# The parts of the recurrent block's weights are made beforehand and kept in DRAM

## The chip, the cores and the metric

The kernel runs on one core of one Trainium2 chip. TensorE (PE) multiplies, VectorE (DVE), ScalarE (ACT) and GpSimd (POOL) work on elements, and SyncE (SP) issues nearly all DMAs, in the order in which they stand in its queue. The metric is the device time of one execution in microseconds (us).

## The reference

Two decoder layers on 512 tokens of 1024 features, in float32. Layer 0 is half a SwiGLU feed-forward, attention, half a feed-forward; layer 1 has a recurrent block (RWKV-7) in place of attention:

```python
for layer in range(DEPTH):                                  # DEPTH = 2
    x = x + 0.5 * swiglu(rms_norm(x, ...), w_gate, w_up, w_down)      # w_*: 1024 x 2816
    h = rms_norm(x, mix_norm[layer])
    x = x + (attention(h, ...) if layer % 2 == 0 else rwkv7_time_mix(h, ...))
    x = x + 0.5 * swiglu(rms_norm(x, ...), ...)

# rwkv7_time_mix
xx = previous_token(h) - h
xr, xw, xk, xv, xa, xg = [h + xx * mix[i] for i in range(6)]
r, k, v = xr @ w_r, xk @ w_k, xv @ w_v                      # each 1024 x 1024
decay = exp(-exp(-softplus(-(w0 + tanh(xw @ w1) @ w2)) - 0.5))
a, g = sigmoid(a0 + (xa @ a1) @ a2), sigmoid(xg @ g1) @ g2
S_t = S_{t-1} (diag(decay_t) - kk_t^T (kk_t a_t)) + v_t k_t^T;  y_t = S_t r_t
return (group_norm(y) + bonus) * g @ w_o
```

## The kernel before

**Stages.** Six stages run one after the other: feed-forward (0,0), attention, feed-forward (0,1), feed-forward (1,0), the recurrent block, feed-forward (1,1). In the trace the first feed-forward takes the time from the start to about 375 us, the recurrent block that from about 1,382 to 1,860 us.

**Weights as parts.** A float32 product is made of three float32r products: each operand is cut into a high and a low part, and `mm3` issues high x high, high x low, low x high (lines 209 to 211). For each piece of weights `_load` issues the DMA into a raw buffer, and `_conv` casts it on ACT (line 181, the high part) and subtracts on DVE (line 182, the low part). A feed-forward piece is 128 partitions x 1,024 columns, 512 KB; a piece of the recurrent block is 128 x 512, 256 KB. There are 4 raw slots and 4 slots for parts. `next_w` hands out the next block of pieces, having converted up to `conv_ahead` (2) pieces beyond it and loaded as far beyond that as there are raw slots. The recurrent block has 75 pieces: the loras' weights `w1`, `a1`, `w2`, `a2`, `g1`, `g2`; two halves of `wk`, `wv` and `wr` of 8 pieces each; 16 pieces of `wo`. The pieces that stay on for long have slots of their own (`wkeep`).

**The recurrent block's front.** `rwkv` normalizes x chunk by chunk (line 967), takes the difference to the previous token (line 1040) and mixes it on DVE (lines 982 and 992), cuts the result on ACT (line 1000) and POOL (line 1001), and multiplies. In the first half of `wk` two loras run along, so each of 8 chunks has three mixes. Then come the second half of `wk`, `wv` with a third lora, `wr`; between them DVE and POOL prepare the heads (`rw_prep`) and DVE inverts triangular blocks (`rw_inverse`). The recursion over 8 chunks of tokens, the group norm and the output product follow.

**Order.** A scheduler sets the order of each engine's instructions from the data they depend on, their place in the program and its own estimate of times. Each engine then runs its queue in that order, and an instruction that waits holds up all behind it. SP's DMAs use 8 semaphores in turn, so a DMA is issued once the eighth before it has landed.

Of the kernel before, what the change touches and what calls it, by code (L numbers as in the profile page):

```python
# [11 lines left out]
F32 = mybir.dt.float32  # L12
# [7 lines left out]
P = 128  # L20
# [10 lines left out]
# pieces of weights on chip: columns, and how many at a time, as they come and as parts  # L31
# [3 lines left out]
# function tables that serve a function, the first where none of them is there  # L35
# [8 lines left out]
class Trunk:  # L44
    def __init__(self, ctx, tc, aps):
# [6 lines left out]
        # constants, x by chunks of features, and weights as they come  # L52
# [8 lines left out]
        # blk[i, j] = 1 within a head  # L61
# [5 lines left out]
        # pieces that stay on for long, and where  # L67
        self.wkeep = {}
        self.wload = self.wconv = self.wpos = 0
# [3 lines left out]
        self.last_mm = self.turned = self.gate = None  # L73
        self.lo_engine = nc.vector
        self.table, self.table_ins, self.preload = None, [], None

    def act(self, out, in_, func, **kw):
        """An activation; those of one function table stay together."""
        nc = self.nc
        serve = TABLES[func]  # L80
        nosync = mybir.DependencyInfo(mybir.DependencyClass.NoSync, mybir.DependencyReason.DATA)
        if self.table not in serve:
            ins = nc.scalar.preload_act_table_set(serve[0])
            for i in self.table_ins:
                self.tc.add_manual_dep(ins.ins, i.name, nosync, reason="table")
            self.table, self.table_ins, self.preload = serve[0], [ins.ins], ins.ins
        ins = nc.scalar.activation(out, in_, func, **kw)  # L87
        self.tc.add_manual_dep(ins.ins, self.preload.name, nosync, reason="table")
        self.table_ins.append(ins.ins)
        return ins  # L90

    def after(self, ins, dep):
        """ins is not to be issued before dep, which it does not depend on."""
# [15 lines left out]
    def c(self, name, shape, v=None):  # L109
        """A constant or scratch that stays."""  # L110
# [25 lines left out]
    def plan(self, *pieces):  # L136
        """A block of pieces, each a list of (first row, first column, [rows, k, c] source)."""
# [4 lines left out]
    def plan_cols(self, w, c0, c1, step=4):  # L142
        """Columns c0..c1 of w, its rows in chunks of 128, some chunks a piece."""
# [3 lines left out]
    def _load(self, i):  # L147
        tag = self.wring[i]
        cols, slots = RINGS[tag]
        if i and "r" in (tag, self.wring[i - 1]) and tag != self.wring[i - 1]:  # L150
            # the last of the other kind's pieces may be there yet
            self.n_load = 0 if tag == "r" else 2
        c0 = self.n_load % slots * cols
        t = self.raw_all[:, c0 : c0 + cols]
        self.n_load += 1
        for r0, c0, src in self.wlist[i]:
# [3 lines left out]
        self.wraw[i] = t  # L160

    def _conv(self, i):
        n = max(c0 + src.shape[1] * src.shape[2] for _, c0, src in self.wlist[i])
        r = max(r0 + src.shape[0] for r0, _, src in self.wlist[i])
        raw = self.wraw.pop(i)[:r]
# [4 lines left out]
        if i not in self.wkeep:  # L170
            # the smaller pieces take the second half in turn, and those that stay the first
# [8 lines left out]
        hi, lo = parts[:, 0, :], parts[:, 1, :]  # L180
        self.nc.scalar.copy(hi[:r, :n], raw[:, :n])  # L181
# [3 lines left out]
        self.wcv[i] = (hi, lo)  # L185

    def prefetch(self, upto, loads=1 << 30):
        """Pieces converted up to and with this one, and loaded as far ahead as there is room."""
# [10 lines left out]
    def next_w(self):  # L199
        """The next block as a list of (high, low) pieces."""  # L200
        i, n = self.wblocks[self.wpos]
        self.wpos += 1
        self.prefetch(i + n - 1 + self.conv_ahead)
        return [self.wcv.pop(j) for j in range(i, i + n)]

    def mm3(self, out, lhs, rhs, start, stop):
        """out (+)= lhs^T rhs, both given as (high, low) float32r parts."""
# [33 lines left out]
    def name_vectors(self, t):  # L241
        """Values by feature, their chunks on columns."""
# [56 lines left out]
    def rms_prep(self, gain):  # L299
        """High and low parts of x * gain, chunk by chunk."""  # L300
# [14 lines left out]
    def rsqrt(self, out, src, scale, eps, t):  # L315
        """out = (src * scale + eps) ** -0.5: exp and ln, then a Newton step; t is scratch."""
# [6 lines left out]
    def newton(self, t, y, src, scale, eps):  # L323
        """t = -0.5 (src * scale + eps) y^2: 1.5 more and it is the step's factor"""
# [42 lines left out]
    def part(w, k, i):  # L367
        """Columns i * 128.. of chunk k, of pieces of four chunks by 256 columns."""
# [3 lines left out]
    def ffn(self, gain, done=lambda c: None):  # L372
# [6 lines left out]
        def gu(b):  # L379
            ps = [self.bank("b", 8) for _ in range(4)]  # L380
            head = 6 if b == 0 else 0
            if head:
                # chunk by chunk as x comes
# [88 lines left out]
    def attn_setup(self):  # L472
        """Masks, selections, and the relative bias as [query, key] tiles."""
        nc = self.nc
        # tri[j, s] = -1 where j >= s
# [5 lines left out]
        # norm weights, one copy per head of a pair; the logits' scale rides on q's  # L481
# [9 lines left out]
    def attn_tables(self):  # L491
        nc = self.nc
        # selections between natural blocks and classes (token 4l + r)
# [13 lines left out]
        # bias: each head's values by distance, then skewed through DRAM  # L507
# [20 lines left out]
    def attn(self, gain):  # L528
# [5 lines left out]
        def scales():  # L534
            st["rstd"] = self.rms_rstd(ssum)
            # the same per token on partitions: natural blocks, then classes
# [8 lines left out]
        def project(w):  # L545
            """A tile of [128 features, tokens] by one piece of weights."""
# [5 lines left out]
        def project_v(by_class, evac):  # L552
            """Tiles of [128 tokens, 256 features]: natural blocks or classes of tokens."""
# [13 lines left out]
        # stick-breaking heads  # L567
# [27 lines left out]
        # dilated heads  # L595
        vd = {}

        def evac_dv(g):
            def f(b, ps, r):
                # of a pair of heads: V, ones, V  # L600
# [59 lines left out]
    def stick(self, q, k, vs, h, out):  # L660
        """One stick-breaking head in [key, query] tiles; a tile covers the queries from its keys on."""
# [3 lines left out]
        for kb in range(3, -1, -1):  # L665
# [9 lines left out]
            # only keys before the query  # L675
# [25 lines left out]
    def dilated(self, t, qk):  # L701
        """Heads 2t and 2t + 1 of the three groups: one softmax over their keys together, by key."""
# [6 lines left out]
        for e in range(2):  # L709
            j, r = 2 * t + e, slice(e * 64, (e + 1) * 64)  # L710
            # group 0: natural blocks, each with the block before it
# [19 lines left out]
            # groups 1 and 2: classes of tokens  # L731
# [11 lines left out]
        def parts(i, src):  # L743
            """High and low parts, and their sum: what the exchange brings across exactly."""
# [5 lines left out]
        # the maximum over all three, by class and by block  # L750
# [43 lines left out]
    def dilated_out(self, t, pts, vd):  # L794
        nc, mm = self.nc, self.nc.tensor.matmul
        dl = self.row("dlo")
        for e in range(2):
# [9 lines left out]
            # V carries ones beside it, which sum the weights  # L807
# [7 lines left out]
    def plan_rwkv(self):  # L815
# [4 lines left out]
        def half(w, h):  # L820
            """512 columns, a chunk of rows a piece."""
# [30 lines left out]
    def rwkv_setup(self):  # L852
# [7 lines left out]
        # sigmoid(z) = (1 + tanh(z / 2)) / 2  # L860
# [8 lines left out]
        # rows i of both halves: i < t, then i <= t  # L869
# [8 lines left out]
        # 0 where a chunk starts  # L878
        self.runs = self.c("runs", [NC, C], 1.0)
        nc.gpsimd.memset(self.runs[:, :, 0:1], 0.0)  # L880
        # a pair's two heads among the 8 of four pairs: sums over a head's features
# [7 lines left out]
    # partitions of values of 8 heads of either four pairs: the keys' norms, the bonus, the group norm  # L889
# [3 lines left out]
    def rwkv_tables(self):  # L893
        """From the 8 heads of four pairs back to their features."""
# [8 lines left out]
        # hidden layers of the loras (2, 2, then all of the rest's products in one), values of heads (2), that table  # L903
# [5 lines left out]
    def head_sums(self, srcs, scales, squares):  # L909
        """Sums of squares over the features of each of 8 heads."""  # L910
# [8 lines left out]
    def head_scale(self, ps, free, scale, eps, floor=None):  # L919
        """(ps * scale + eps) ** -0.5 for sums [8 heads, tokens], as high and low parts."""  # L920
        nc = self.nc
        ss, y, t = (z[:8] for z in free)
        if floor is not None:
            nc.vector.tensor_scalar(out=ss, in0=ps, scalar1=floor, scalar2=None, op0=ALU.max)
            # the logarithm's range does not reach down to the floor
# [16 lines left out]
    def head_spread(self, n, m):  # L942
        """A pair's values per head on all features of the head."""
# [6 lines left out]
    def rwkv(self, gain):  # L950
# [11 lines left out]
        # h in x's place  # L962
# [14 lines left out]
        def mixed(i, c, tag="xm", bufs=9, dh=None):  # L977
            """High and low parts of h (1 - mix[i]) + (previous token's h) mix[i]."""
# [16 lines left out]
            if tag == "xr":  # L995
                # where a lora's weights were
# [21 lines left out]
        def evac_v(half, ps):  # L1018
            # The recursion is linear in V's features, and the group norm takes their mean off what
            # comes of it: it is taken off V. The bonus has V as it is.  # L1020
# [14 lines left out]
        def less(t, c, ts):  # L1035
            """The previous token's h less this one's."""
# [7 lines left out]
        def started():  # L1044
            """Half of the tokens at a time: the first chunk, and products on it."""
# [14 lines left out]
        def project(half, xm, evac, natural, i_mix=None, loras=(), wl=None):  # L1060
            """Half of a projection's columns, the chunks of rows outermost."""
# [71 lines left out]
        # mix rows: r, w, k, v, a, g  # L1133
# [20 lines left out]
        # the receptances' mix is made twice: there is no room to keep it  # L1154
# [9 lines left out]
        # high, high, low: against high, low, high parts  # L1164
# [9 lines left out]
    def rw_norm(self, sg):  # L1174
        """Norms of the keys' directions, bounded below by 1e-12."""
# [6 lines left out]
    def rw_prep_all(self, sg):  # L1182
        """Four pairs of heads, their steps in turn."""
        # a pair: [kk P(t-1), later y | r P(t) | [k / P, -kk a / P] (2) | ties, later inverse]
# [5 lines left out]
    def rw_prep(self, m):  # L1190
        """Scaled k, kk and kk * a of a pair of heads, and what a chunk's tokens owe each other."""
# [18 lines left out]
        # decay = exp(-exp(-1/2) sigmoid(z)); its products within a chunk, and their inverses  # L1210
# [8 lines left out]
        # the key's direction, -kk / 2; k (1 + (a - 1) ka); -kk a  # L1219
# [18 lines left out]
        # [k / P, -kk a / P], k in its head's half of the rows to come  # L1238
# [6 lines left out]
        # the keys' ties to later directions within a chunk, rows i in the half that is not the head's own  # L1245
# [9 lines left out]
        # the 32-blocks on the diagonal go out for inversion  # L1255
# [11 lines left out]
    def rw_prep2(self, sg):  # L1267
        """The receptances' part of it: r P, and each head's bonus."""
# [309 lines left out]
```

## Time and profile before

| | |
|---|---|
| time, median of 3 runs | 2236.47 us (2234.1 to 2237.83) |
| profiled execution, first to last instruction | 2236.3 us |
| PE busy | 2160.0 us (97%) |
| DVE busy | 1223.1 us (55%) |
| ACT busy | 784.1 us (35%) |
| POOL busy | 283.1 us (13%) |
| moved by DMA | 204.21 MB, mean 91 GB/s |

The profile is of one execution. Its span of 2236.3 us is 0.2 us from the median of the runs, and no separate time of that execution stands beside it. Busy time of PE is not PE at its peak: matmuls are pipelined, so of two products on PE the number of them in a stretch says more than the busy time. The granted clock (PEclk) is 1.00 where the chip lets TensorE run at 2.4 GHz, and 0.50 would be 1.2 GHz throughout.

### The profile page before, as it was taken

The numbers are of one execution on the slowest core, as the hardware profiler recorded it, in microseconds if no ns is written. First come the engines' busy times: TensorE is split into PE (matmuls) and PEld (weight loads), VectorE is DVE, ScalarE is ACT, GpSimd is POOL, SyncE is SP. The second block draws the span as 40 slices with busy tenths as digits, with TensorE's granted clock in tenths as the row PEclk, the third lists the DMA queues.
The fourth block names the chain that finished last, engine by engine and source line by source line (L and its number), as shares of the span: only waits on it lengthen the run. The fifth ranks groups of instructions, "written<-read, shape, count | busy, mean of one in ns | idle before, by whom it ended". The sixth has DMA issues, their size and how long they took to land. (4 is left out here: it accounts for less than half of the span.)

```text
span 2236.3 us, 28431 instructions
## 1 busy us (share of the span) xinstructions
PE 2160.0 (97%) x11489; PEld 1737.6 (78%) x11489; DVE 1223.1 (55%) x1618; ACT 784.1 (35%) x1223; POOL 283.1 (13%) x286
## 2 busy tenths in 40 slices
PE   8999999999999999999999998789888999999999
PEld 6888887768988888888888886566657767888887
DVE  5444445467385444446444445999876456444443
ACT  4322324454234222224222224465533334322222
POOL 3000001120010000001000002663461101000000
PEclk9999999999899999999999998999988899999999
DMA  5232333411023333233232332123423232232322
GB/s 173 76 113 93 97 100 97 119 38 52 20 71 102 99 97 109 76 113 94 77 116 90 103 104 86 47 85 115 128 66 89 61 113 85 82 116 85 109 90 66
DMA packets 229868, 204.21 MB, mean 91 GB/s; under 512 B 39651, under 2 KB 215931, under 8 KB 229736
## 3 DMA queue, kind: packets, MB, share of 16 engines
q1 hardware_dynamic: 227624, 200.29, 30.2%
q10 hardware_dynamic: 2112, 2.10, 0.3%
q8 instruction: 90, 1.47, 0.3%
q14 instruction: 42, 0.34, 0.0%
HBM read 188.68 MB, written 15.51 MB: 91 GB/s over the span
## 5 line engine op out<-in xcount | busy, mean ns | idle before, releaser
L182 DVE TENSOR_TENSOR parts<-const,parts 128x1024 fp32r<-128x1024 f32 (+2 forms) x394 | 428.8, 1094 | 350.2 <-ACT parts L181 341.0
L181 ACT CAST parts<-const 128x1024 fp32r<-128x1024 f32 (+2 forms) x394 | 357.4, 910 | 573.9 <-PE b L210 469.6
L210 PE MATMUL b<-xg,parts 128*128 128x512 f32 x1408 | 549.2, 390 | 0.0
L209 PE MATMUL b<-xg,parts 128*128 128x512 f32 x1408 | 547.0, 391 | 1.6 <-ACT xg L308 1.1
L211 PE MATMUL b<-xg,parts 128*128 128x512 f32 x1408 | 548.3, 390 | 0.0
L209 PEld LDWEIGHTS b<-xg,parts 128*128 128x128 f32 x1408 | 264.7, 188 | 57.7 <-ACT xg L308 1.5
L210 PEld LDWEIGHTS b<-xg,parts 128*128 128x128 f32 x1408 | 264.9, 188 | 56.4 <-issue 1.0
L211 PEld LDWEIGHTS b<-xg,parts 128*128 128x128 f32 x1408 | 264.7, 188 | 55.4 <-DVE parts L182 0.3
L211 PE MATMUL b<-act,parts 128*128 128x512 f32 x704 | 273.3, 389 | 0.0
L210 PE MATMUL b<-act,parts 128*128 128x512 f32 x704 | 273.2, 389 | 0.0
L209 PE MATMUL b<-act,parts 128*128 128x512 f32 x704 | 272.4, 390 | 0.0
L296 POOL TENSOR_TENSOR ssum<-ssum,sq 128x512 f32<-128x512 f32 x41 | 59.2, 1445 | 1191.4 <-ACT sq L295 526.5
L426 DVE SCALAR_TENSOR_TENSOR const<-b,const 128x512 f32<-128x512 f32 x128 | 87.3, 687 | 124.5 <-PE b L211 124.5
L211 PEld LDWEIGHTS b<-act,parts 128*128 128x128 f32 x704 | 132.2, 188 | 27.4
L210 PEld LDWEIGHTS b<-act,parts 128*128 128x128 f32 x704 | 132.2, 188 | 27.4
L209 PEld LDWEIGHTS b<-act,parts 128*128 128x128 f32 x704 | 132.2, 188 | 27.2
L411 DVE TENSOR_TENSOR u<-b,rstd 128x512 f32<-128x512 f32 x88 | 60.4, 690 | 167.1 <-PE b L211 166.9
L214 ACT CAST act<-u 128x512 fp32r<-128x512 f32 x88 | 54.6, 622 | 268.6 <-DVE u L412 268.6
L87 ACT ACTIVATE g<-g 128x512 f32<-128x512 f32 x88 | 55.0, 629 | 188.0 <-DVE g L406 188.0
L406 DVE TENSOR_TENSOR g<-b,rstd 128x512 f32<-128x512 f32 x88 | 60.4, 691 | 108.1 <-PE b L211 107.8
L215 DVE TENSOR_TENSOR act<-u,act 128x512 fp32r<-128x512 f32 x88 | 60.6, 689 | 37.2 <-ACT act L214 36.7
L412 DVE TENSOR_TENSOR u<-u,g 128x512 f32<-128x512 f32 x88 | 60.5, 691 | 2.7
(356 smaller groups left out, 2728.0 us busy)
## 6 DMA issues: line engine op xcount, KB each, us to landing
const<-in_ffn_w_gate_dram SPq DMA_DIRECT2D x88, 512.0 KB
const<-in_ffn_w_up_dram SPq DMA_DIRECT2D x88, 512.0 KB
const<-in_ffn_w_down_dram SPq DMA_DIRECT2D x64, 512.0 KB
const<-in_ffn_w_down_dram SPq DMA_DIRECT2D x48, 256.0 KB
const<-in_attn_w_in_dram SPq DMA_DIRECT2D x24, 512.0 KB
const<-in_rw_wk_dram SPq DMA_DIRECT2D x16, 256.0 KB
const<-in_rw_wv_dram SPq DMA_DIRECT2D x16, 256.0 KB
const<-in_rw_wr_dram SPq DMA_DIRECT2D x16, 256.0 KB
```

The lines of the kernel that those rows point to most:

```text
L87: ins = nc.scalar.activation(out, in_, func, **kw)
L181: self.nc.scalar.copy(hi[:r, :n], raw[:, :n])
L182: self.lo_engine.tensor_tensor(out=lo[:r, :n], in0=raw[:, :n], in1=hi[:r, :n].bitcast(F32), op=ALU.subtract)
L209: self.after(mm(out, lhs[0], rhs[0], start=start, stop=False), self.gate)
L210: mm(out, lhs[0], rhs[1], start=False, stop=False)
L211: self.last_mm = mm(out, lhs[1], rhs[0], start=False, stop=stop)
L215: self.nc.vector.tensor_tensor(out=lo, in0=t, in1=hi.bitcast(F32), op=ALU.subtract)
L296: nc.gpsimd.tensor_tensor(out=ssum, in0=ssum, in1=sq, op=ALU.add)
L406: nc.vector.tensor_tensor(out=g, in0=ps[i], in1=rstd, op=ALU.mult)
L411: nc.vector.tensor_tensor(out=u, in0=ps[2 + i], in1=rstd, op=ALU.mult)
L412: nc.vector.tensor_tensor(out=u, in0=u, in1=gs[i], op=ALU.mult)
L426: nc.vector.scalar_tensor_tensor(out=self.x[c], in0=ps, scalar=0.5, in1=self.x[c], op0=ALU.mult, op1=ALU.add)
```

## The change

A new pair of steps, called parking here, takes the 75 pieces two by two. `park` loads two pieces into a buffer of its own (`praw`), cuts them into parts in another (`pparts`) with one cast on ACT (line 200) and one subtraction on DVE (line 201), and stores high and low parts to DRAM, one DMA a piece (line 204). Both buffers are double. `next_w` calls it at every second block while the flag `parking` is set, in stages 2 and 3. In the recurrent block `_load` does nothing, and `_conv` issues one DMA of 512 KB that brings both parts into their slot (line 226); no cast and no subtraction is left there. All else of the diff is comments taken out. (In the rows of order below, lines of the changed kernel are its own: 167 is the load that was 159, 230 the subtraction that was 182, 1031 the mix that was 982.)

```diff
+        self.parked_w, self.park_ops, self.park_turn = {}, [], 0
+        self.parking = False
     def _load(self, i):
         tag = self.wring[i]
+        if tag == "r":
+            return
...
+    def plan_parks(self, every):
+        small = [i for i, tag in enumerate(self.wring) if tag == "r"]
+        self.park_ops = [small[j : j + 2] for j in range(0, len(small), 2)]
+        self.park_every = every
+    def park_some(self):
+        self.park_turn += 1
+        if self.park_ops and self.park_turn % self.park_every == 0:
+            self.park(self.park_ops.pop(0))
+    def park(self, which):
+        nc = self.nc
+        raw, parts = self.t("praw", [2, S], 2), self.t("pparts", [2, 2, S], 2, F32R)
+        dr = self.dram.tile([len(which), P, 2, S], F32, name=f"parts{which[0]}")
+        spans = []
+        for q, i in enumerate(which):
+            self._fill(i, raw[:, q])
+            spans.append(self._extent(i))
...
+        for r, q, c in spans:
+            hi, lo, src = parts[:r, 0, q, c], parts[:r, 1, q, c], raw[:r, q, c]
+            nc.scalar.copy(hi, src)
+            nc.vector.tensor_tensor(out=lo, in0=src, in1=hi.bitcast(F32), op=ALU.subtract)
+        for q, i in enumerate(which):
+            r, n = self._extent(i)
+            nc.sync.dma_start(dr[q, :r, :, :n], parts[:r, :, q, :n].bitcast(F32))
+            self.parked_w[i] = dr[q, :r, :, :n]
     def _conv(self, i):
...
+        if i in self.parked_w:
+            self.nc.sync.dma_start(parts[:r, :, :n].bitcast(F32), self.parked_w.pop(i))
+            return
+        raw = self.wraw.pop(i)[:r]
         self.nc.scalar.copy(hi[:r, :n], raw[:, :n])
     def next_w(self):
         self.prefetch(i + n - 1 + self.conv_ahead)
+        if self.parking:
+            self.park_some()
...
+    t.plan_parks(2)
     for i in range(start, stop + 1):
+        t.parking = i in (2, 3)
```

SP's queue in the first feed-forward, before, from the third block of columns to the first `down` loads (`const` holds the raw slots):

```order
L159 DMA const<-in_ffn_w_gate_dram 128x4x256 x2
L159 DMA const<-in_ffn_w_up_dram 128x4x256 x2
L159 DMA const<-in_ffn_w_gate_dram 128x4x256 x2
L159 DMA const<-in_ffn_w_up_dram 128x4x256 x2
L159 DMA const<-in_ffn_w_down_dram 128x4x256
L159 DMA const<-in_ffn_w_down_dram 128x2x256
```

The same place now, from the `gate` loads of the fourth block of columns to the first `down` load (`parts_` with a number is a pair's place in DRAM):

```order
L167 DMA const<-in_ffn_w_gate_dram 128x4x256 x2
L204 DMA parts_5181<-pparts 256x1x512 x2
L167 DMA praw<-in_rw_wk_dram 128x512 x2
L204 DMA parts_5302<-pparts 256x1x512 x2
L167 DMA praw<-in_rw_wk_dram 128x512 x2
L167 DMA const<-in_ffn_w_up_dram 128x4x256 x2
L204 DMA parts_5441<-pparts 256x1x512 x2
L167 DMA praw<-in_rw_wk_dram 128x512 x2
L167 DMA const<-in_ffn_w_down_dram 128x4x256
```

The parking, written in stages 2 and 3, depends on nothing that comes before them, and the scheduler has moved all 38 pairs into stage 0: the first load of a pair is number 17 in SP's queue, and the last store stands between the 54th and the 55th of that stage's 72 weight loads.

DVE's queue in the first half of `wk`, before, over two of the 8 chunks:

```order
L982 SCALAR_TENSOR_TENSOR mx<-dh,const 128x512
L182 TENSOR_TENSOR parts<-const,parts 128x512
L982 SCALAR_TENSOR_TENSOR mx<-dh,const 128x512
L967 SCALAR_TENSOR_TENSOR const<-const,rstd 128x512
L182 TENSOR_TENSOR parts<-const,parts 128x512
L982 SCALAR_TENSOR_TENSOR mx<-dh,const 128x512 x2
L1039 TENSOR_SCALAR dh<-const 128x1
L1040 TENSOR_TENSOR dh<-const 128x511
L182 TENSOR_TENSOR parts<-const,parts 128x512 x2
```

The same stretch now:

```order
L1031 SCALAR_TENSOR_TENSOR mx<-dh,const 128x512 x2
L1016 SCALAR_TENSOR_TENSOR const<-const,rstd 128x512
L1031 SCALAR_TENSOR_TENSOR mx<-dh,const 128x512
L1088 TENSOR_SCALAR dh<-const 128x1
L1089 TENSOR_TENSOR dh<-const 128x511
L1031 SCALAR_TENSOR_TENSOR mx<-dh,const 128x512 x2
```

The conversions are gone and the mixes follow each other; the rest of the order is nearly the same.

ACT's queue at the very start holds casts of the parking ahead of the last chunks of x (now; `xg` is x times the gain, line 357):

```order
L357 ACTIVATE xg<-b,const 128x512
L344 ACTIVATE sq<-const 128x512
L200 CAST pparts<-praw 128x1024
L357 ACTIVATE xg<-b,const 128x512
L344 ACTIVATE sq<-const 128x512
```

Before, the two pairs of rows followed each other there, without the cast.

## Rows read from the trace of the kernel before

**Rows 1.** Busy time by stretch (us; PE, PEld, DVE, ACT, POOL, PEclk, DMA share, GB/s)
```profile
40.00:340.00 300.00, 300.00 (x1326) 248.38 (x1325) 137.24 (x168) 84.11 (x102) 0.00 (x0) 1.00 0.33 99
1382.00:1440.00 58.00, 36.59 (x139) 25.77 (x139) 57.02 (x66) 21.70 (x38) 41.31 (x26) 0.84 0.16 50
1440.00:1480.00 40.00, 40.00 (x151) 25.27 (x150) 31.16 (x38) 34.42 (x60) 18.52 (x13) 0.97 0.24 70
1480.00:1580.00 100.00, 84.12 (x430) 59.99 (x428) 95.75 (x148) 47.38 (x78) 51.37 (x36) 0.94 0.36 111
1580.00:1620.00 40.00, 38.94 (x389) 29.22 (x390) 29.97 (x38) 27.88 (x47) 20.23 (x16) 0.89 0.48 125
1720.00:1860.00 140.00, 132.01 (x1337) 97.96 (x1338) 75.47 (x113) 55.60 (x132) 14.65 (x16) 0.90 0.29 86
```

**Rows 2.** Groups on DVE by form, 40 to 340 us (busy, mean ns | idle before)
```profile
L182 DVE TENSOR_TENSOR parts<-const,parts 128x1024 fp32r<-128x1024 f32 x48 | 58.7, 1223 | 66.4 <-ACT parts L181 66.4
L182 DVE TENSOR_TENSOR parts<-const,parts 128x512 fp32r<-128x512 f32 x12 | 8.2, 682 | 0.0
```

**Rows 3.** Groups on DVE and POOL by form, 1,382 to 1,620 us
```profile
L182 DVE TENSOR_TENSOR parts<-const,parts 128x512 fp32r<-128x512 f32 x46 | 45.5, 994 | 6.3 <-ACT parts L181 5.9
...
L1001 POOL TENSOR_TENSOR xl<-mx,xl 128x512 fp32r<-128x512 f32 x16 | 26.0, 1639 | 2.6 <-ACT xl L1000 2.6
```

**Rows 4.** Line 182 alone in five of the stretches (DVE busy, PEclk, DMA share, GB/s)
```profile
1382.00:1440.00 58.00, 11.94 (x8) 0.84 0.16 50
1440.00:1480.00 40.00, 10.47 (x11) 0.97 0.24 70
1480.00:1580.00 100.00, 19.01 (x20) 0.94 0.36 111
1580.00:1620.00 40.00, 7.87 (x10) 0.89 0.48 125
1720.00:1860.00 140.00, 16.88 (x22) 0.90 0.29 86
```

**Rows 5.** The stretch in which the recurrent block starts
```profile
1380.00:1400.00 20.00, 10.22 (x43) 8.24 (x42) 18.12 (x31) 9.11 (x17) 11.19 (x6) 0.66 0.17 54
```

**Rows 6.** Groups on PE by form, 1,480 to 1,580 us
```profile
L210 PE MATMUL rm<-parts,xm 128*128 128x512 f32 x64 | 26.6, 415 | 3.7 <-DVE parts L182 3.7
...
L1250 PE MATMUL rq<-heads 64*64 64x64 f32 x128 | 5.6, 232 | 3.3 <-DVE heads L1233 2.5 <-POOL heads L1243 0.8
```

**Rows 7.** The chain that ended last, end of the recurrent block
```profile
1846.95 1.19 DVE parts L182
```

**Rows 8.** SP's issues of weights in the first feed-forward (start, us, issues)
```profile
27.46 2.73 SPq L159 DMA_DIRECT2D const<-in_ffn_w_gate_dram  x2
...
48.77 3.09 SPq L159 DMA_DIRECT2D const<-in_ffn_w_gate_dram  x2
...
70.57 33.56 SPq L159 DMA_DIRECT2D const<-in_ffn_w_down_dram  x8
...
255.53 3.51 SPq L159 DMA_DIRECT2D const<-in_ffn_w_up_dram  x2
```

**Rows 9.** Short stretches, columns as in Rows 1
```profile
51.50:52.00 0.50, 0.50 (x4) 0.42 (x3) 0.00 (x0) 0.00 (x0) 0.00 (x0) 1.00 0.91 318
52.00:52.50 0.50, 0.50 (x4) 0.42 (x3) 0.00 (x0) 0.00 (x0) 0.00 (x0) 1.00 0.04 14
8.00:12.00 4.00, 2.88 (x9) 2.04 (x8) 3.47 (x6) 2.59 (x5) 1.29 (x3) 1.00 1.10 348
1381.00:1384.00 3.00, 1.06 (x4) 0.61 (x4) 1.12 (x5) 2.50 (x6) 0.00 (x0) 1.00 0.98 313
```

**Rows 10.** Group on ACT by form, 40 to 340 us
```profile
L181 ACT CAST parts<-const 128x1024 fp32r<-128x1024 f32 x48 | 50.6, 1054 | 101.6 <-PE b L210 101.6
```

**Rows 11.** ACT in order of time, start of the kernel
```profile
22.04 0.69 ACT L308 ACTIVATE xg<-b,const 128x512 fp32r<-128x512 f32 x1 [0.84 <-DVE const L236]
...
32.84 0.69 ACT L308 ACTIVATE xg<-b,const 128x512 fp32r<-128x512 f32 x1 [4.63 <-DVE const L236]
...
46.43 1.05 ACT L181 CAST parts<-const 128x1024 fp32r<-128x1024 f32 x1
```

**Rows 12.** DVE in order of time, third block of columns
```profile
65.69 0.69 DVE L406 TENSOR_TENSOR g<-b,rstd 128x512 f32<-128x512 f32 x1 [2.29 <-PE b L211]
```

**Rows 13.** SP in order of time, a store to DRAM and the load that reads it
```profile
1580.41 0.32 SPq L1311 DMA_DIRECT2D tout<-inv  x1
...
1584.60 1.41 SPq L1317 DMA_DIRECT2D const<-tout  x2
```

More of the change, by code (lines that the diff above doesn't have):

```diff
@@ L148, in _load @@
         tag = self.wring[i]
+        if tag == "r":
+            return
         cols, slots = RINGS[tag]
-        if i and "r" in (tag, self.wring[i - 1]) and tag != self.wring[i - 1]:
-            self.n_load = 0 if tag == "r" else 2
+        if i and self.wring[i - 1] == "r":
+            self.n_load = 0
         c0 = self.n_load % slots * cols
@@ L155, in _load, with _fill @@
         self.n_load += 1
+        self._fill(i, t)
+        self.wraw[i] = t
+    def _fill(self, i, t):
         for r0, c0, src in self.wlist[i]:
@@ L159, in _load, with _extent, _conv @@
             self.nc.sync.dma_start(dst, src)
-        self.wraw[i] = t
-    def _conv(self, i):
+    def _extent(self, i):
         n = max(c0 + src.shape[1] * src.shape[2] for _, c0, src in self.wlist[i])
         r = max(r0 + src.shape[0] for r0, _, src in self.wlist[i])
-        raw = self.wraw.pop(i)[:r]
+        return r, n
+    def plan_parks(self, every):
[14 more added lines that the diff above has]
+            spans.append(self._extent(i))
+        if len(set(spans)) == 1 and spans[0][1] == S and len(which) == 2:
+            spans = [(spans[0][0], slice(0, 2), slice(0, S))]
+        else:
+            spans = [(r, slice(q, q + 1), slice(0, n)) for q, (r, n) in enumerate(spans)]
+        for r, q, c in spans:
[6 more added lines that the diff above has]
+            self.parked_w[i] = dr[q, :r, :, :n]
+    def _conv(self, i):
+        r, n = self._extent(i)
         tag = self.wring[i]
@@ L180, in _conv @@
         hi, lo = parts[:, 0, :], parts[:, 1, :]
+        self.wcv[i] = (hi, lo)
+        if i in self.parked_w:
+            self.nc.sync.dma_start(parts[:r, :, :n].bitcast(F32), self.parked_w.pop(i))
+            return
+        raw = self.wraw.pop(i)[:r]
         self.nc.scalar.copy(hi[:r, :n], raw[:, :n])
@@ L184, in _conv @@
         )
-        self.wcv[i] = (hi, lo)
     def prefetch(self, upto, loads=1 << 30):
```

## Prediction

> **What bounds the kernel now.** I read first the page's busy shares and slices, then the windows by stage, then the groups by form in the two stages that change, and last the short orders in time in which one load, one cast or one store is seen. PE is busy for 97% of the span, but not alike everywhere. In the first feed-forward it never stops: 1,326 matmuls in 300 us, 300 / 1,326 = 0.226 us each, while DVE has 137 us of work, ACT 84, and DMA moves 99 GB/s [rows 1]. There the other engines and DMA have room, and only PE's own work sets the time. In the recurrent block's front it is DVE: 57.0 of 58 us from 1,382 on and 95.8 of 100 us from 1,480 on, with PE at 36.6 and 84.1 [rows 1]. PE waits there for what DVE makes, and in DVE's order the conversions stand between the mixes, so what DVE is spared there can move the end.
>
> **What is removed.** DVE loses the 75 subtractions of line 182 and ACT the 75 casts. A subtraction of 128 x 512 takes 0.682 us in the first feed-forward, where POOL does nothing, and 0.994 us in the front, where POOL works beside it [rows 2, 3]. Stage by stage, with line 182's share from [rows 4] and what is late next from [rows 1]:
> - 1,382 to 1,440: 8 subtractions, 11.9 us of DVE. DVE falls to 45.1 of 58; next are POOL with 41.3 and PE with 36.6. The clock was 0.84 over the stretch and 0.66 where the block starts, with 10.2 us of matmuls in 20 [rows 1, 5]. I take 10 of the 11.9: -10.
> - 1,440 to 1,480: 10.5 us, but PE is busy all 40 us and its 151 matmuls at 0.226 us are 34 us of work: at most -6, I take -2.
> - 1,480 to 1,580: 20 subtractions, 19.0 us. DVE falls to 76.7 of 100; of PE's 430 matmuls 128 are of 64 columns (5.6 us), and the other 302 are at most 68 us at 0.226: some 74 us of work [rows 6]. I take three quarters: -14.
> - 1,580 to 1,620: 7.9 us, but PE is busy 38.9 of 40: -1.
> - 1,720 to 1,860: 16.9 us, DVE at 75.5 of 140 and PE at 132. One subtraction stands in the chain at the end, with 1.19 us [rows 7]; in its place stands a load of 512 KB, which from issue to data took some 3.2 us (48.77 to 52.0, where the rate falls from 318 to 14 GB/s) [rows 8, 9]. I take 0.
>
> Sum: -10 - 2 - 14 - 1 = -27. The bounds: all of line 182 from 1,382 to 1,620 is 11.9 + 10.5 + 19.0 + 7.9 = 49 us, and about 45 if PE's own work holds back 4; the small end is about -8, if only the first stretch gives anything and loads that are twice as large take some back.
>
> **What the added loads cost in the block.** A piece now is one DMA of 512 KB in place of one of 256 KB. The rate in the front was 50 to 125 GB/s at a share of 0.16 to 0.48 [rows 1]; 75 pieces add 19.4 MB, at most 60 GB/s more on average over 330 us. That fits under 313 GB/s, the rate of a stretch of pure stores at a share of 0.98 [rows 9]. The raw ring is gone, so a piece is loaded only when one of 4 slots is free, not ahead of that. I cost it at nothing, since a slot comes free two pieces ahead of use; where it isn't covered the piece is late by up to 3.2 us less the cover.
>
> **What parking costs.** The order shows that all 38 pairs go into the first feed-forward, between 18 us and the point at which the loads of 255.53 us were issued before [rows 8]. Per full pair: two loads (0.52 MB), one ACT cast of 128 x 1,024 at 1.05 us, one DVE subtraction at 1.22 us, two stores (1.05 MB) [rows 2, 10]. With the shorter lora pieces there are 42 casts and 42 subtractions: about 44 us of ACT and 51 us of DVE. DVE goes from 137 to at most 188 of 300 us and ACT from 84 to 128 [rows 1]: hidden by PE, if the queues' order fits.
>
> DMA is the narrow place. Up to the last store SP's queue has 19.4 MB of pair loads, 38.8 MB of stores and 54 weight loads (26.2 MB); with 0.5 MB of small ones 84.9 MB, of which 2.7 are before 18 us. So 82.2 MB stand in 255.5 - 18 = 237.5 us: 346 GB/s where nothing may be late. The slack is what the weights are early: the load issued at 27.46 us was converted at 46.43 us, some 15 us after it had landed [rows 8, 11]; of the time from that cast to the first product's result (DVE takes it at 65.69 us, 24 matmuls or 5.4 us after their start) some 13 us more can go [rows 11, 12]. An estimate from these: 15 + 13 less 1 = 27 us, so 82.2 MB / 264.5 us = 311 GB/s is the rate below which PE waits. What the trace shows of rates: 318 GB/s within one load, 348 over 4 us of loads at a share of 1.10, 313 for stores at 0.98 [rows 9]. That is so near that I count a stall: at 303 GB/s, 3% under the stores' rate for gaps in SP's queue, 82.2 / 0.303 = 271.3 us, 7 us too long. At 320 GB/s it is 0; at 270, 304.4 us and +40.
>
> The start adds one more. Casts of the parking stand on ACT ahead of the last chunks of x (before at 22.04 and 32.84 us) [rows 11]; they wait for loads that SP issues at about 19 us, which land behind 1.5 MB of weights. PE has other columns to do meanwhile, so of a wait of up to 10 us (its bound) I count +3, with 0 as the other end.
>
> A store to DRAM and the load that reads it stood 4.19 us apart (1,580.41 and 1,584.60) [rows 13]. Each pair's stores must land before its parts buffer is used again, two pairs later, that is 2 x 264.5 / 38 = 13.9 us; with loads that land in some 6.7 us (2 MB in flight at 313 GB/s), 1.05 and 1.22 us a pair takes 9.0 us and has 4.9 us left for waits. The Trainium skill, "DMA: Bandwidth & Descriptors", section "Latency and other measured facts", speaks against the change here: each DMA carries about 2 us of fixed cost, most of it the receipt of the write, and most in DRAM. Were 2 us unhidden in each of 38 pairs, that would be 76 us, less the slack some 50; the row of 4.19 us shows a store with its receipt inside what is left, so I keep to the rate.
>
> **Sum.** -27 + 7 + 3 = -17 on the profiled execution's 2,236.3 us, which is the runs' median to 0.2 us: 2,219 us.
>
> **Rivals.**
> - *The first feed-forward becomes DMA-bound (slower).* ACT and DVE run in order, and a park's cast or subtraction stands behind work that waits for PE, as DVE waited 2.29 us for line 406 and ACT 4.63 us for a chunk of x [rows 11, 12]. If a pair waits 7 us and not 4.9, a pair holds one of two buffers for 9 + 7 = 16 us; 38 x 16 / 2 = 304 us, 270 GB/s: +40 in place of +7. Time 2,236.3 - 27 + 40 + 3 = 2,252. It decides below 285 GB/s, where gain and loss are level (82.2 / 0.285 = 288 us: +24 and +3 against -27). For it: 346 GB/s without slack is near the most ever seen. Against it: pieces are early by 15 us, and the DMAs are large.
> - *The front doesn't give the time back.* POOL (51.4 of 100) and PE, and the parts' loads behind waiting stores in SP's queue, take DVE's place, and only some 8 of 27 us come: 2,236.3 - 8 + 10 = 2,238, no change. For it: of the 22 conversions after 1,720 us none is worth anything. Against it: DVE is busy 95.8 of 100 us.
> - *More gain.* Line 182 and POOL's line 1001 (1.64 us) run side by side [rows 3]; if POOL's part shrinks too, all but 10 of the 49 us come back, and with parking hidden it is -39 + 3: 2,200. The Trainium skill, "SBUF — State Buffer", section "SBUF: two separate sides", says that DVE with two operands in SBUF and GpSimd lock each other out fully; the 0.994 against 0.682 us agree in sign. By it the subtractions of the front would free POOL by up to their whole busy time, more than this rival takes.
>
> **Chances.** Forecast (2,205 to 2,231) 0.48; DMA-bound 0.27; not given back 0.12; more gain 0.13. Some 0.2%, 4.5 us, is what a measurement of this kernel tells from no change: 2,232 to 2,241. Faster is the forecast, more gain and none of the others, 0.61; the same takes 0.10 of "not given back"; slower is DMA-bound and its remaining 0.02, 0.29. The range 2,196 to 2,258 leaves 0.05 below and 0.12 above.
>
> **What would show it.** Right: between 18 and 260 us the rate is 300 to 320 GB/s, PE stalls by less than 12 us there, and the first feed-forward ends some 10 us later; the front from 1,382 us on is some 27 us shorter, with DVE still the busiest and its mixes back to back; the output product's part unchanged. Wrong: a rate below 285 GB/s with PE waiting for casts of line 229; a first feed-forward without any stall; or a front in which PE or ACT waits for DMAs of line 226.

## The result and the profile after

The changed kernel takes 2,218.67 us (median of 4 runs, 2,217.48 to 2,220.63) against 2,237.01 us before: ratio 0.9923, 95% interval 0.991 to 0.9937. The forecast was 2,219. The total came out right, but three of its terms did not, and a fourth was missing; their errors nearly cancel, which is luck. The page of after, its span and the last two lines of the 40 slices (share of DMA in tenths, rate):

```profile
span 2217.2 us, 28598 instructions
...
DMA  9999733411013233333232323255652243232332
GB/s 318 348 344 339 258 100 98 117 48 46 27 45 112 95 100 98 93 109 92 84 109 76 114 92 124 88 170 161 196 154 69 53 155 105 86 107 84 109 95 62
```

The parking fills the first four and a half slices. The windows of after, columns as in [rows 1]; five of the first feed-forward, then the stretches that answer to those of [rows 1]:

```profile
18.00:40.00 22.00, 20.75 (x94) 16.17 (x93) 15.23 (x18) 13.31 (x19) 8.77 (x6) 1.00 1.00 336
40.00:100.00 60.00, 60.00 (x267) 49.64 (x266) 42.89 (x53) 31.17 (x40) 0.00 (x0) 1.00 1.01 351
100.00:160.00 60.00, 60.00 (x266) 49.69 (x265) 36.72 (x42) 24.16 (x27) 0.00 (x0) 1.00 1.00 348
160.00:220.00 60.00, 60.00 (x266) 49.69 (x265) 38.69 (x47) 27.24 (x35) 0.00 (x0) 1.00 0.98 333
220.00:260.00 40.00, 40.00 (x179) 33.10 (x178) 24.46 (x28) 15.46 (x18) 0.00 (x0) 1.00 0.98 343
...
1387.00:1440.00 53.00, 37.75 (x137) 27.04 (x137) 51.86 (x57) 17.09 (x30) 39.43 (x26) 0.81 0.26 86
1440.00:1480.00 40.00, 40.00 (x154) 25.57 (x154) 23.30 (x29) 32.12 (x53) 13.49 (x14) 0.99 0.43 141
1480.00:1570.00 90.00, 76.73 (x403) 54.98 (x402) 76.52 (x126) 33.65 (x51) 43.92 (x32) 0.93 0.53 178
1720.00:1830.00 110.00, 104.95 (x1130) 76.63 (x1126) 51.89 (x80) 37.14 (x100) 9.64 (x11) 1.00 0.35 104
```

DMA is saturated for 240 us (share 0.98 to 1.01, 333 to 351 GB/s) and PE still never waits from 40 us on: 267 and 266 matmuls in 60 us. PE's one wait for the parking is at the start. ACT of after stands at a cast of the parking that waits for its load, the last chunk of x behind it, and PE at that chunk (first fence ACT, second PE, in order of time):

```profile
33.55 1.05 ACT L200 CAST pparts<-praw 128x1024 fp32r<-128x1024 f32 x1 [4.04 <-DMA praw<-in_rw_wk_dram]
34.51 0.68 ACT L357 ACTIVATE xg<-b,const 128x512 fp32r<-128x512 f32 x1
```

```profile
35.24 0.96 PE L258 MATMUL b<-xg,parts 128*128 128x512 f32 x3 [1.11 <-ACT xg L357]
```

To see where the 19 us between the two profiled executions arise, take the same instruction in both traces. From the timelines (start in us; L with a number is the line in the kernel before):

| instruction | before | after | later by | in this stretch |
|---|---|---|---|---|
| first bias row, DVE L513, end of the first feed-forward | 376.91 | 378.12 | 1.2 | +1.2 parking |
| first scores of attention, DVE L575 | 391.04 | 395.14 | 4.1 | +2.9 |
| DVE L771, middle of attention | 535.69 | 541.24 | 5.5 | +1.4 |
| SP L280, start of the recurrent block | 1380.45 | 1385.49 | 5.0 | -0.5 |
| first head prepared, DVE L1213, behind the mixes | 1465.68 | 1463.76 | -1.9 | -6.9 |
| second inverse done, DVE L1344 | 1727.87 | 1720.32 | -7.5 | -5.6 |
| last head's output, DVE L1471 | 1848.06 | 1828.84 | -19.2 | -11.7 |

### The profile page after: what moved, and what is told of

Read it like the earlier page. It is cut to its first block, busy times and chain, and to the rows that moved or that the text cites. A ratio compares the mean times of both kernels' runs of the same rounds, so it can differ in the third digit from the quotient of the medians.

```text
span 2217.2 us, 28598 instructions
## 1 busy us (share of the span) xinstructions
PE 2155.1 (97%) x11489; PEld 1735.9 (78%) x11489; DVE 1211.0 (55%) x1585; ACT 781.1 (35%) x1190; POOL 274.5 (12%) x286
## 4 chain that ended last, share of the span: by engine, by line
PE 88%; DVE 8%; DMA 3%; issue 1%; ACT 1%; POOL 0%; SPq 0%; DVEq 0%; ACTq 0%; POOLq 0%
PE b L259 21%; PE b L260 21%; PE b L258 21%; PE am L259 3%; PE am L258 3%; PE am L260 3%; DVE mx L1031 1%; DVE const L1352 1%; PE rm L258 1%; PE rm L259 1%; PE rm L260 1%; PE ra L1412 1%; DVE inv L1356 1%; PE wo L258 1%; DMA const<-in_ffn_w_up_dram 1%; PE wo L259 1%
## 5 line engine op out<-in xcount | busy, mean ns | idle before, releaser
L230 DVE TENSOR_TENSOR parts<-const,parts 128x1024 fp32r<-128x1024 f32 (+2 forms) x320 | 362.4, 1139 | 305.5 <-ACT parts L229 304.2
L229 ACT CAST parts<-const 128x1024 fp32r<-128x1024 f32 (+2 forms) x320 | 312.5, 977 | 515.8 <-PE b L259 445.1
L264 DVE TENSOR_TENSOR act<-u,act 128x512 fp32r<-128x512 f32 x88 | 60.6, 689 | 34.8 <-ACT act L263 34.2
```

The source lines that it names most:

```text
L230: self.lo_engine.tensor_tensor(out=lo[:r, :n], in0=raw[:, :n], in1=hi[:r, :n].bitcast(F32), op=ALU.subtract)
L264: self.nc.vector.tensor_tensor(out=lo, in0=t, in1=hi.bitcast(F32), op=ALU.subtract)
```

## The experiments

Twelve kernels ran. Ratios are of the time to that of the kernel before on the same chip (2,237.3 us in the first four, 2,238.7, 2,239.6 and 2,237.6 in the next groups).

**Parking without use.** The block loads and converts its pieces itself.

```diff
-        if i in self.parked_w:
+        if i in self.used_parked:      # empty
```

> All 38 pairs are parked as in the changed kernel, but the recurrent block loads and converts its pieces itself, as before; what was parked is read by nobody. Theory (parking is free but for 1.1 us at the start, since SP's transfers ran at 343 to 351 GB/s): 2236.5 + 1 = 2238 us, and the first feed-forward ends 1 us late. If the two falls of TensorE's clock in attention (+3.0 and +1.4 us) belong to parking, they stand here too: 2242. Rival (parking moves the rest of the order and is itself a gain): below 2232.

Measured 2,311.3 us, 1.0334 (1.0311 to 1.0357): a fault of the experiment. The new `_load` sets the raw slot back to 0 behind every "r" piece, so all 75 raw loads went through one slot. Its first feed-forward is valid: PE 1.2 us late at 40 us and no later at 360. With before's rule for the slots it was run again:

> All 38 pairs parked as in the changed kernel and read by nobody; the recurrent block loads and converts as before, now with its four raw slots (the first kernel of this kind had by mistake one). Theory (parking costs 1.2 us at the start, and 2.3 us of clock in attention come with it, as in the first four stages of that run): 2240 us. Rival (parking itself changes what follows): below 2234 or above 2245.

Measured 2,242.72 us, 1.002 (1.0009 to 1.0031): parking costs 4 to 5 us with attention's share, and gives nothing by itself.

**Use without parking.**

```diff
+        self.park_ops = [small[j : j + 2] for j in range(0, 8, 2)]
...
+        if tag == "r":
+            place = self.small[2 + self.small.index(i) % 6]
+            self.nc.sync.dma_start(parts[:r, :, :n].bitcast(F32), self.parked_w[place][:r, :, :n])
```

> Only 4 pairs are parked, in the second feed-forward, and every one of the 75 pieces is loaded from six of their places: 512 KB each, as in the changed kernel, but with wrong weights for most pieces. Theory (the gain is the conversions taken from DVE and ACT in the recurrent block): the block is 24 us shorter as in the changed kernel and nothing is paid for parking: 2212 us, 2217 if attention loses its 4.4 us here as well. Rival (9 of the 24 us are TensorE's clock in the recursion, which fell before at 1720 to 1760 us and not after, by chance of the order): 2221 to 2226.

Measured 2,214.24 us, 0.9906 (0.9892 to 0.992): the gain is in the block. Of its five runs one took 2,222.7, the others 2,213.8 to 2,215.8; the trace, and so its row in the table below, is of the one. The rival named TensorE's clock, and this does not rule it out: the mean granted clock was 0.983 to 0.986 in the four, about 0.977 in the kernel before.

**Parking where it is written.** The loads get an order dependency on the matmul ahead of the call.

```diff
-            self._fill(i, raw[:, q])
+            self._fill(i, raw[:, q], self.last_mm)
```

> The changed kernel, with each pair's loads ordered behind the matmul that comes before its call, so that parking lies in the second and third feed-forward. Theory: DMA has as much room there and the start is not touched, so 2217.5 us (1.1 less than the changed kernel); the rate in these stages is some 200 to 250 GB/s and PE does not wait. Rival (spread over two stages, stores and loads of the parking stand in SP's queue ahead of weights in two stages and at three stage boundaries): 2222 or more.

Measured 2,225.48 us, 0.9945 (0.9932 to 0.9958). It costs 7 us more than parking in the first feed-forward: the rival's number, but not its way, since the three feed-forwards keep their lengths. The difference is in the block (table below): 447.9 us against 440.9, with PE idle for 54.7 and 45.2 of them. Why PE waits longer there stays open.

**No subtractions.**

```diff
         self.nc.scalar.copy(hi[:r, :n], raw[:, :n])
+        if tag == "r":
+            self.wcv[i] = (hi, hi)
+            return
```

> The kernel before, with the 75 subtractions of the recurrent block's pieces left out: the high part stands in for the low one, so the products there are wrong. ACT's casts and the 256 KB loads stay. Theory (DVE is what bounds the block, ACT is not): nearly all of the 24 us come, 2214 us. Rival (ACT's 75 casts, and the wait of loads on the raw ring, carry half): 2224.

Measured 2,233.25 us, 0.9972 (0.9957 to 0.9987), in two groups of runs: four at 2,223.7 to 2,225.0, with a mean granted clock of 0.982 or 0.983, and eight at 2,231.5 to 2,238.8, with 0.977 to 0.980. My theory that DVE's time is nearly all of the gain falls. In its trace, which is of the second group, the front is 9.9 us shorter than before, but the recursion longer by 4.7.

**Casts.** So the next two took ACT's casts out as well, of the late pieces and of all; their high part is loaded from four parked pairs.

```diff
+        if tag == "r" and i >= self.late:          # the other run: all pieces
+            self.nc.sync.dma_start(hi[:r, :n].bitcast(F32), self.parked_w[place][:r, 0, :n])
+            self.wcv[i] = (hi, hi)
+            return
```

> As the run without subtractions, and of the last pieces of the block (g2 and wo, used in the recursion's second half and behind it) the casts are left out too: their high part is loaded as it is. All other pieces keep raw load and cast. Theory (ACT's waits for those loads, 10 to 12 us in the traces with casts, hold up the recursion): 2214 to 2218 us, with the stretch from the second inverse to the output product at 105 to 110 us. Rival (the casts of the block's front carry the difference): 2224 to 2233, as without subtractions alone.

> As the run with parts alone (4 pairs parked), but only the high part is loaded, 256 KB a piece, and stands in for the low one: no casts, no subtractions, and transfers of the old size; products of the recurrent block are wrong. Theory (what the run without subtractions lacked are ACT's casts, which wait at the head of ACT's queue for their loads between the two halves of the recursion): 2214 to 2217 us. Rival (the gain needs loads of finished parts in 512 KB pieces or their order): 2222 or more.

Measured 2,220.34 us, 0.9926 (0.9906 to 0.9945), without the late casts, and 2,225.56 us, 0.9947 (0.9929 to 0.9966), without any. The first is clear of the run without subtractions alone (the intervals do not meet): 0.0046 of 2,238 us, 10 us, for the casts of the 20 last pieces. Part of that is the clock: among runs at 0.982 to 0.984 the medians are 2,224.4 and 2,218.5 us, 6 us apart. The second shows no gain from the casts of the front, but it ran at 0.972 to 0.980, the first at 0.979 to 0.984, so the two do not settle what these casts are worth.

**POOL.** Line 1050 (1001 before) makes the mixed inputs' low parts on POOL.

```diff
-            nc.gpsimd.tensor_tensor(out=m[:, 1, :], in0=t, in1=m[:, 0, :].bitcast(F32), op=ALU.subtract)
+            nc.vector.tensor_tensor(out=m[:, 1, :], in0=t, in1=m[:, 0, :].bitcast(F32), op=ALU.subtract)
```

First the line was left out, the high part returned twice; then moved to DVE for all six inputs, for three, and in the kernel before:

> The changed kernel, with the subtractions of line 1050 on POOL left out (the high part of the mixed inputs stands in for the low one; wrong products in the block). Theory (three quarters of the DVE time freed in the front did not come, since DVE and POOL now slow each other: mixes went from 1131 to 1422 ns): mixes fall to some 0.8 us and the front is 15 us shorter or more: 2204 or less. Rival (PE and the chain through DVE bound the front by themselves): 2212 or more.

> The changed kernel with line 1050's subtraction (the low part of the mixed inputs) on DVE in place of POOL; nothing is left out. From the traces: a mix takes 0.78 us with POOL idle and 1.42 us beside it, and a subtraction of 128 x 512 on DVE 0.68 us, so mix and subtraction on DVE take 1.46 us, where the mix alone takes 1.42 now. Theory (DVE and POOL hold each other up, so POOL's help in the front is worth next to nothing): the mixes' stretch stays within 4 us of the changed kernel's 52.8 us, and the time within 6 us of 2218.7. Rival (POOL's work is a real relief of DVE): the 37 or more subtractions of the front add 0.68 us each, 25 us: 2240.

> The changed kernel with line 1050's subtraction on DVE for w, v and g and on POOL for r, k and a; nothing is left out. Theory: as above, no more than 4 us to either side of 2218.7, since what POOL is spared DVE does in the same time. Rival (some mixture keeps both engines busy without waiting for one another): 2212 or less.

> The kernel before, with only the subtraction of the mixed inputs moved from POOL to DVE (line 1001); weights are converted in the block as before. Theory (what DVE gains from an idle POOL is the same with the conversions in the block: every DVE instruction beside POOL's is some 0.3 us longer): 14 us less than before, 2225. Rival (it works in the changed kernel only since the conversions left room on DVE; here 25 us of subtractions come on top of a DVE that is busy for 96 of 100 us): 2236 or more.

Measured 2,203.76 us, 0.9848 (0.9826 to 0.987), without the subtraction; 2,204.27, 0.9844 (0.983 to 0.9857), with all of them on DVE; 2,209.34, 0.9866 (0.9853 to 0.988), with half; 2,234.04, 0.9978 (0.9965 to 0.9991), in the kernel before. Doing the work on DVE costs no more than leaving it out. Both theories for the moves fail: I had expected no more than 6 and 4 us, and they gain 14 and 9, with the mixes' stretch 6 us shorter in the first. The mean clock does not explain it: 0.980 to 0.984 with all on DVE, 0.981 to 0.983 in the changed kernel. In the kernel before the gain is some 4 us only (the interval allows 2 to 8): there the mixes end 7 us earlier too, but at the second inverse 1.5 us of that are left. DVE is still busy for 91.4 of 100 us from 1,480 on (95.8 without the move), and the granted clock up to that point is 0.88 (0.91 without); which of the two takes the rest back is not shown.

**The best version found.** Three products of the heads' preparation go from POOL to DVE too.

```diff
-        nc.gpsimd.tensor_tensor(out=k, in0=kx, in1=k, op=ALU.mult)
+        nc.vector.tensor_tensor(out=k, in0=kx, in1=k, op=ALU.mult)
...
-            nc.gpsimd.tensor_tensor(out=bk[hs, :, 1 - hh, :], in0=ch(a)[hs], in1=ch(pi)[hs], op=ALU.mult)
+            nc.vector.tensor_tensor(out=bk[hs, :, 1 - hh, :], in0=ch(a)[hs], in1=ch(pi)[hs], op=ALU.mult)
...
-            nc.gpsimd.tensor_tensor(out=rp, in0=r, in1=rp, op=ALU.mult)
+            nc.vector.tensor_tensor(out=rp, in0=r, in1=rp, op=ALU.mult)
```

> The changed kernel with the mixed inputs' subtraction on DVE and with POOL's three products of the heads' preparation (lines 1276, 1292, 1324; 31 of them in the front, 1.6 us each) on DVE too; nothing is left out. Theory (DVE does each in some 0.4 to 0.7 us and its own are no longer held up, so the preparation's stretch gets shorter): 2198, 6 us below the run with the mixed inputs alone. Rival (here POOL's products run beside DVE work that does not suffer, or DVE is the bound): 2204 or more.

Measured 2,196.99 us, 0.9824 (0.9806 to 0.9842): faster than both kernels, with nothing left out.

The block's stretches in the profiled executions (us; lines of before): from its start (the last DMA of line 280 there) to the start of the last mix of line 982; from the same start to the end of the second inverse; and from there to the last product of line 1470, which takes in the second recursion:

| kernel | mixes | second inverse | rest |
|---|---|---|---|
| before | 58.4 | 347.4 | 117.7 |
| parked, not used (2nd) | 58.8 | 347.0 | 113.0 |
| before, mixes on DVE | 51.0 | 345.9 | 111.6 |
| no subtractions | 51.2 | 337.5 | 122.5 |
| no subtractions, no late casts | 51.2 | 332.1 | 109.8 |
| no conversions at all | 51.2 | 336.3 | 115.5 |
| use without parking | 51.2 | 337.4 | 109.0 |
| changed kernel | 52.5 | 334.8 | 106.1 |
| parked in stages 2 and 3 | 51.2 | 331.8 | 116.1 |
| changed, POOL's line left out | 34.8 | 311.2 | 109.8 |
| changed, half on DVE | 51.8 | 327.8 | 103.5 |
| changed, on DVE | 46.3 | 319.6 | 107.4 |
| best version | 46.3 | 312.4 | 107.3 |

## Why the prediction was right, and where it was not

**The front, forecast -27, measured -12.5** (-6.9 and -5.6): right in kind, mis-sized. From the block's start to the second inverse PE stood idle for 56.7 us before and for 42.0 after, at a clock of 0.91 and 0.92. In the first stretch DVE was the bound and still is (51.9 of 53 us); from 1,480 to 1,570 neither DVE nor PE is full any more (76.5 and 76.7 of 90). I took the freed time as gain and did not ask what becomes of POOL's instructions beside it. The costliest groups on DVE from 1,382 to 1,620 us, of before and then of after (busy, mean ns | idle):

```profile
L982 DVE SCALAR_TENSOR_TENSOR mx<-dh,const 128x512 f32<-128x512 f32 x23 | 25.3, 1131 | 0.0
...
L1215 DVE TENSOR_TENSOR_SCAN heads<-const,heads 128x512 f32<-128x512 f32 x8 | 9.5, 1212 | 0.1
L1040 DVE TENSOR_TENSOR dh<-const 128x511 f32<-128x511 f32 x7 | 8.8, 1264 | 0.0
```

```profile
L1031 DVE SCALAR_TENSOR_TENSOR mx<-dh,const 128x512 f32<-128x512 f32 x23 | 31.9, 1422 | 0.0
...
L1264 DVE TENSOR_TENSOR_SCAN heads<-const,heads 128x512 f32<-128x512 f32 x8 | 12.6, 1602 | 0.1
...
L1089 DVE TENSOR_TENSOR dh<-const 128x511 f32<-128x511 f32 x7 | 10.9, 1563 | 0.0
```

The same mixes take 0.29 us more each. These three lines alone give back 6.6 + 3.1 + 2.1 = 11.8 us of the 45.5 us that line 182 had there [rows 3]: with the conversions gone, DVE's mixes meet POOL's subtractions more often. The same view without POOL's line, and with it on DVE:

```profile
L1031 DVE SCALAR_TENSOR_TENSOR mx<-dh,const 128x512 f32<-128x512 f32 x23 | 16.7, 779 | 0.2
```

```profile
L1031 DVE SCALAR_TENSOR_TENSOR mx<-dh,const 128x512 f32<-128x512 f32 x23 | 17.4, 800 | 0.2
...
L1050 DVE TENSOR_TENSOR xl<-mx,xl 128x512 fp32r<-128x512 f32 x16 | 11.1, 704 | 0.0
```

A mix with its subtraction takes 0.80 + 0.70 = 1.50 us on DVE alone; beside POOL the mix alone took 1.42, and the subtraction 1.65 us on POOL. The Trainium skill, "SBUF — State Buffer", section "SBUF: two separate sides", has DVE with two operands in SBUF and GpSimd shut each other out; 0.78 against 1.42 us agrees. My rival "more gain" named this pair, but with the sign that POOL would run faster; in the row it named POOL kept its 1.64 us [rows 3] (1.65 after), and DVE paid. POOL's other 36 subtractions of 128 x 512 in the front did get shorter, from 60.3 to 51.8 us.

**The recursion, forecast 0, measured -11.7**: wrong. I weighed line 182's time against a load of 512 KB, and overlooked two things: ACT's casts, which wait for their loads at the head of ACT's queue, and TensorE's clock. ACT and DVE of before, in order of time, about the second inverse and behind it:

```profile
1725.95 1.27 ACT L181 CAST parts<-const 128x512 fp32r<-128x512 f32 x2 [3.28 <-DMA const<-in_rw_wo_dram]
1727.25 0.58 ACT L1344 COPY heads<-rq 32x512 f32<-32x512 f32 x1
...
1740.39 0.62 ACT L181 CAST parts<-const 128x512 fp32r<-128x512 f32 x1 [2.96 <-DMA const<-in_rw_wo_dram]
1742.32 0.62 ACT L181 CAST parts<-const 128x512 fp32r<-128x512 f32 x1 [1.30 <-DMA const<-in_rw_wo_dram]
1742.84 0.58 ACT L1460 COPY heads<-rq 128x512 f32<-128x512 f32 x1
```

```profile
1735.98 0.69 DVE L182 TENSOR_TENSOR parts<-const,parts 128x512 fp32r<-128x512 f32 x1 [7.44 <-ACT parts L181]
```

The copies of the inverse and of the heads stand behind casts that wait for `wo`. After, a load goes from SP straight to the slot, and only the product that needs it waits. But these waits hardly reach PE. The last stretch of the table, columns as in [rows 1], of before, after, parked in stages 2 and 3, no subtractions, and no subtractions with no late casts:

```profile
1727.90:1845.60 117.70, 113.72 (x1143) 83.00 (x1142) 59.51 (x91) 43.89 (x113) 11.41 (x13) 0.91 0.29 88
1720.30:1826.40 106.10, 102.86 (x1113) 75.26 (x1114) 49.25 (x77) 35.35 (x97) 9.64 (x11) 1.00 0.35 103
1715.60:1831.70 116.10, 112.44 (x1282) 84.33 (x1281) 52.26 (x79) 38.98 (x109) 11.98 (x13) 1.00 0.34 100
1717.20:1839.70 122.50, 114.66 (x1231) 84.11 (x1226) 54.26 (x81) 47.02 (x123) 12.00 (x14) 0.94 0.31 93
1714.10:1823.90 109.80, 107.46 (x1228) 79.40 (x1224) 52.77 (x81) 37.67 (x105) 10.44 (x12) 1.00 0.29 86
```

PE is idle for 4.0 us before and for 3.2 after, so waits make up 0.8 of the 11.6 us. What changed is the granted clock, 0.91 and 1.00. What that is worth can be seen in before, where the same eight matmuls stand once in a stretch at the upper level and once at the lower:

```profile
1700.98 1.16 PE L1368 MATMUL ra<-const,heads 128*128 128x128 f32 x8
1726.53 2.07 PE L1368 MATMUL ra<-const,heads 128*128 128x128 f32 x8
```

```profile
1700.00:1705.00 5.00, 4.49 (x94) 3.84 (x92) 4.79 (x11) 1.64 (x6) 1.05 (x1) 1.00 0.01 3
1725.00:1730.00 5.00, 4.23 (x36) 3.70 (x36) 1.94 (x3) 3.33 (x7) 1.05 (x1) 0.50 0.32 101
```

At a mean of 0.91, 18% of 117.7 us, 21 us, lie at the lower level; 1 - 1.16 / 2.07 = 0.44 of that is 9 us, an estimate. In the changed kernel none is lost there. So nearly all of this term is the clock. Why it fell in before is not shown; waits that casts caused may have had a part in it. The pair of runs without subtractions, with and without the late casts, shows that casts can cost PE more: of 12.7 us, PE's waits are 5.5 (7.8 against 2.3), and the clock of 0.94 by the same estimate 6. Where parking is in stages 2 and 3 the clock is 1.00 and the stretch takes 116.1 us, but there more of the block's work is left for it, 1,282 matmuls against 1,113.

The clock counts for the whole, too. Its mean over a run was about 0.977 in the kernel before and 0.981 to 0.983 in the changed one. That is 4.6% of 2,237 us and 3.6% of 2,219 at the lower level, 23 us less, and by the same estimate up to 10 of the 18 us gained. The forecast costed the conversions by the time that DVE and ACT spend on them, and no term of it stands for the clock.

**The parking's stall, forecast +7, measured 0; its start, forecast +3, measured +1.2.** The step that failed is the rate. I took 303 GB/s from 3 us that I called pure stores [rows 9]. They were not, since SP issued loads of `wk` around the store:

```profile
1379.86 0.33 SPq L159 DMA_DIRECT2D const<-in_rw_wk_dram  x1
1380.45 0.38 SPq L280 DMA_DIRECT2D park<-const  x1
1381.06 0.33 SPq L159 DMA_DIRECT2D const<-in_rw_wk_dram  x1
```

In the parking loads and stores together ran at 333 to 351 GB/s for 240 us, as the 348 over 4 us [rows 9] could have told. The mean from 18 to 260 us was 343, so the 346 that is needed without any slack was all but met. The estimate of slack was not put to the test. The fixed cost of a DMA that the Trainium skill, "DMA: Bandwidth & Descriptors", names in "Latency and other measured facts" does not show as a stall: the share stays at 0.98 to 1.01, so other transfers fill the time.

**Attention, not forecast, +4.3.** It is TensorE's clock, not DMA. The window of 383 to 393 us, before and after:

```profile
383.00:393.00 10.00, 10.00 (x45) 8.25 (x44) 6.94 (x13) 1.68 (x4) 0.00 (x0) 1.00 0.21 72
```

```profile
383.00:393.00 10.00, 10.00 (x33) 8.14 (x33) 6.22 (x13) 1.78 (x5) 0.00 (x0) 0.67 0.29 94
```

The work comes 1.2 us later (first row of the table), and at a mean clock of 0.67 33 matmuls run where 45 did. Over the table's third stretch the clock falls again: from 526 to 536 us it was 1.00 before and 0.83 after.

**The sum.** Forecast -27 + 10 = -17; measured -12.5 - 11.7 + 1.2 + 4.3 - 0.5 = -19.2 in the profiled pair. The front's overestimate, 14.5 us, is made up by the recursion (11.7) and by parking (8.8 cheaper), less attention. That is luck, and by its own signs the prediction failed: it asked for a stall of PE and 300 to 320 GB/s in the first feed-forward, a front some 27 us shorter, and an output part that does not change.

## What to carry to other kernels

Before an instruction is taken off a bound engine, look at its neighbours' durations with and without another engine beside them: here much of the freed time went into longer instructions beside POOL, and work given to POOL can cost DVE as much as it spares it. A conversion that waits for a load at the head of an in-order queue holds up all behind it; whether that costs time is read from the waits of the engine that bounds the stretch. Compare the granted clock of each stretch before a gain is put down to a wait: here up to 10 of the 18 us gained are its. Work without dependencies goes where the scheduler finds room: ask the order, not the code, in which stage it lands, and sum the bytes there.

## What the runs showed of the hardware

- DMA held 333 to 351 GB/s at a share of 0.98 to 1.01 over 240 us, loads and stores mixed, with no wait of PE from 40 us on.
- Where the first feed-forward passes into attention, the granted clock went with when it does. Of the 14 profiled kernels, the five whose first bias row came at 376.7 to 377.1 us had 1.00 in the window from 383 to 393 us; the nine in which it came at 376.0, or at 378.0 and later, had 0.50 to 0.87. What the chip decides by is not settled by these runs.
- A mix of 128 x 512 on DVE took 0.78 us without POOL's subtractions and 1.13 to 1.42 us beside them.
- Eight matmuls of 128 x 128 took 1.16 us where the granted clock was 1.00 and 2.07 us where it was 0.50. The same program ran in two groups by the clock: without subtractions, 2,223.7 to 2,225.0 us at 0.982 or 0.983, and 2,231.5 to 2,238.8 at 0.977 to 0.980.
